# Cross-attention of a streaming encoder layer: queries projected features-first, and a fixed order for the passage to the products with wo

## The chip, the cores and the metric

The kernel runs on one core of a Trainium2 chip. The metric is the device time of one execution in microseconds (us); lower is better. Differences of less than 0.2% are taken as no change.

## The reference

One layer on 1024 tokens of width 1024, all in float32: a mixer (forgetting attention and gated linear attention side by side) with its output product w_out, a cross-attention to 256 memory tokens with 4 heads of 256, and an MLP with squared ReLU.

```python
h = h + parallel_mixer(rms_norm(h, norm_mix_g), w_in, ..., w_out)
h = h + memory_cross_attention(rms_norm(h, norm_xattn_g), rms_norm(mem, norm_mem_g),
                               xattn_wq, xattn_wkv, xattn_q_norm_g, xattn_k_norm_g, xattn_wo)
u = jax.nn.relu(rms_norm(h, norm_mlp_g) @ mlp_w1)
h = h + (u * u) @ mlp_w2

def memory_cross_attention(hn, memn, wq, wkv, q_norm_g, k_norm_g, wo):
    q = rms_norm((hn @ wq).reshape(B, S, XATTN_HEADS, XATTN_HEAD_DIM), q_norm_g)
    k, v = jnp.split(memn @ wkv, 2, axis=-1)
    k = rms_norm(k.reshape(B, M, XATTN_HEADS, XATTN_HEAD_DIM), k_norm_g)
    v = v.reshape(B, M, XATTN_HEADS, XATTN_HEAD_DIM)
    s = jnp.einsum('bshd,bmhd->bhsm', q, k) / math.sqrt(XATTN_HEAD_DIM)
    p = jax.nn.softmax(s, axis=-1)
    o = jnp.einsum('bhsm,bmhd->bshd', p, v).reshape(B, S, D_MODEL)
    return o @ wo
```

## The kernel before

Five engines work beside each other, each on its own list of instructions: TensorE (PE in the profile), VectorE (DVE), ScalarE (ACT), GpSimd (POOL), and SyncE (SP), which issues most transfers. The program is written in Python with pools of buffers; a scheduler that simulates the engines while the program is built sets the order of the instructions on each engine. An instruction waits on its engine until its operands are there and its output's buffer is free, and everything behind it on that engine waits with it.

Every float32 product is made of three products of halves. An operand is split into a high part (one copy on ACT) and a low part (operand minus high part, on DVE): `wh`, `wl` for weights, `sh`, `sl` for h, `th`, `tl` for the attention weights, `oh`, `ol` for the cross-attention's output. `gemm` (L105) then issues, for each block k of 128 summed features, high times high (L110), high times low (L111 or L112) and low times high. Where the text says "a product" of 128x512, one such PE instruction is meant.

The residual stream `h` lies in SBUF with features on the partitions: 8 blocks of 128 features, 1024 tokens each. `project_out` (L842) makes the last products with w_out, first for tokens 0 to 511 (half 0), then for half 1. For each of 8 feature blocks it loads `hr`, the part computed earlier, adds it on DVE (L860), squares the result on ACT (L169) and accumulates the squares on POOL (L170); `token_squares` (L172) sums the squares over features by four transposes on PE, and the token factors (among them `hev`) follow on POOL. After that comes `xattn` (L963), then `project_o_rest` (L891) with the rest of the products with wo, and `mlp`.

`xattn` works on half n of wq's columns (two heads) and a pair u of token tiles of 128:
- `weights(n)` loads half of wq in four transfers of 512 KB into two raw buffers and splits it (L99, L100), and loads the keys kT and values vm.
- `queries(n, u)` splits h of a token tile (`split_tile`, L823 and L824, one instruction each for 128x1024), and multiplies with the tokens as the stationary operand: 24 products 128x512. The result has tokens on the partitions, so `head_rstd` squares it on ACT, sums on DVE and takes the factor on POOL; DVE scales q, four transposes (L1003) turn it, and it is split into qh and ql.
- `attend(n, u)` makes for each token tile 12 score products 128x256, the maximum (DVE), the exponentials (ACT), the normalisation (POOL) and four transposes, and then for both tiles together 24 value products `pv` 128x256. The result `o` is split and stored to memory in four transfers of 256 KB (L1043).

The units run as (0,0) to (0,3), (1,2), (1,3), (1,0), (1,1); `attend` of a unit is written behind `queries` of the next. `project_o_first` (L883) loads o of half 1 in eight transfers of 512 KB (L872, L873), splits half of wo and makes four output blocks of 24 products.

Of the kernel before, what the change touches and what calls it, by code (L numbers as in the profile page):

```python
# [51 lines left out]
class Layer:  # L52
# [52 lines left out]
    def gemm(self, ps, lh, ll, rh, rl, start=True, stop=True, **kw):  # L105

        mm = self.nc.tensor.matmul
        n = len(lh)
        for k in range(n):
            mm(ps, lh[k], rh[k], start=start and k == 0, stop=False, **kw)  # L110
            mm(ps, lh[k], rl[k], start=False, stop=False, **kw)  # L111
            mm(ps, ll[k], rh[k], start=False, stop=stop and k == n - 1, **kw)  # L112
# [86 lines left out]
    def build(self):  # L199
        with ExitStack() as st:  # L200
# [19 lines left out]
            with ExitStack() as mx:  # L220
# [11 lines left out]
                self.h = self.T(self.open(st, "h", side="right"), [P, KT, S], F32, "h")  # L232
                self.project_out()
# [14 lines left out]
    def consts(self, cp):  # L248
# [9 lines left out]
        self.mhalf = self.T(cp, [P, 8], F32, "mhalf")  # L258
        nc.vector.memset(self.mhalf, -0.5)
# [554 lines left out]

    def split_tile(self, sp, srcs, kt=KT):

        nc = self.nc
        sh = self.T(sp, [P, kt, P], F32R, "sh")
        sl = self.T(sp, [P, kt, P], F32R, "sl")
        k = 0  # L820
        for src in srcs:
            w = src.shape[1]
            nc.scalar.activation(sh[:, k:k + w, :], src, AF.Copy)  # L823
            nc.vector.tensor_tensor(sl[:, k:k + w, :], src, f(sh[:, k:k + w, :]), ALU.subtract)  # L824
            k += w
        return [sh[:, k, :] for k in range(kt)], [sl[:, k, :] for k in range(kt)]

# [14 lines left out]
    def project_out(self):  # L842

        nc = self.nc
        with ExitStack() as st:
            banks = self.two(self.mmp, 2, self.open(st, "mm3b", 4, space=PSUM), 4)
            xp = self.open(st, "xp3", 3)
            self.acc = [self.T(xp, [P, 512], F32, f"acc{i}", bufs=1) for i in range(2)]
            ks = range(4), range(2, 4)
            Ws = [self.wsplit(self.w_out[ks[n][0] * P:512, n * 512:(n + 1) * 512], None, lo_pool=0) for n in range(2)]  # L850
            for half in range(2):
# [10 lines left out]
                c = slice(4 * half, 4 * half + 4)  # L862
                self.token_squares(half, self.hv[:, c])
                nc.gpsimd.tensor_scalar(self.hev[:, c], self.hv[:, c], EPS, None, ALU.mult)
                nc.gpsimd.tensor_tensor(self.hr[:, c], self.hv[:, c], self.mhalf[:, 0:4], ALU.pow)

    def load_o(self, op, half):

        oh = self.T(op, [P, KT, 512], F32R, "oh")
        ol = self.T(op, [P, KT, 512], F32R, "ol")  # L870
        for k in (slice(k, k + 2) for k in range(0, KT, 2)):
            self.nc.sync.dma_start(f(oh[:, k, :]), self.od[:, 0, half, k, :])  # L872
            self.nc.sync.dma_start(f(ol[:, k, :]), self.od[:, 1, half, k, :])  # L873
        self.O[half] = [oh[:, k, :] for k in range(KT)], [ol[:, k, :] for k in range(KT)]

    def o_block(self, W, n, half, i, ps, out=None):

        c = slice(i * P, (i + 1) * P)
        self.gemm(ps, *([w[:, c] for w in w_] for w_ in W), *self.O[half])
# [3 lines left out]
    def project_o_first(self):  # L883

        self.ost, self.O = ExitStack(), {}
        self.load_o(self.open(self.ost, "op0", side="right"), 1)
        self.Wo = self.wsplit(self.wo[:, 0:512], None)
        for i in range(4):
            self.o_block(self.Wo, 0, 1, i, self.T(self.mmp, [P, 512], F32, "mm"))

    def project_o_rest(self, mx):  # L891
# [5 lines left out]
        with ExitStack() as st:  # L897
            xp = self.open(st, "xp")
# [5 lines left out]
            op1 = self.open(st, "op1")  # L904
            wst = st.enter_context(ExitStack())
            wx = self.open(wst, "wx", 7)
            banks = self.two(self.mmp, 2, self.open(st, "mm5", 4, space=PSUM), 4)
# [3 lines left out]
            self.load_o(op1, 0)  # L911
# [3 lines left out]
            self.acc = [self.T(p, [P, 512], F32, "acc") for p in (self.open(mx, "acc", side="right"), xp)]  # L915
# [34 lines left out]
            self.A = next(self.W1)  # L950
# [12 lines left out]
    def xattn(self):  # L963
        nc = self.nc
        with ExitStack() as st:
            kvp = [None, self.open(st, "kv41")]
            qp = self.open(st, "q4", 3)
            qnp = self.open(st, "qn4", 2)
            pp = self.open(st, "p4", 3)
            ptp = self.open(st, "pt4", 2)  # L970
            mmp, trp = self.mmp, self.trp
            kst = ExitStack()
            kvp[0] = self.open(kst, "kv40")
            sst = ExitStack()
            sp = self.open(sst, "sp", 2, side="right")
            sps = self.open(st, "s4", 2, space=PSUM)
            pvp = self.open(st, "pv4", 2, space=PSUM)
            v2 = lambda ap: ap.rearrange("p (h d) -> p h d", h=2)
            v4 = lambda ap: ap.rearrange("p (h d) -> p h d", h=4)
            Ws, KV = {}, {}  # L980

            def weights(n):
                Ws[n] = self.wsplit(self.wq[:, n * 512:(n + 1) * 512], C_XAT)
                kT = self.T(kvp[n], [P, 2, 4, M], F32R, "kT")
                nc.sync.dma_start(f(kT), self.kTd[:, :, 4 * n:4 * n + 4, :])
                vm = self.T(kvp[n], [P, 2, 2, 512], F32R, "vm")
# [3 lines left out]
            def queries(n, u):  # L990
                qh = self.T(qp, [P, 2, 4, P], F32R, "qh")
                ql = self.T(qp, [P, 2, 4, P], F32R, "ql")
                for i in range(2):
                    t = 2 * u + i
                    A = self.split_tile(sp, (self.h[:, :, t * P:(t + 1) * P],))
                    ps = self.T(mmp, [P, 512], F32, "mm")
                    self.gemm(ps, *A, *Ws[n])
                    qn = self.T(qnp, [P, 512], F32, "qn")
                    r = self.head_rstd(ps, qn, 2, self.hev[:, t:t + 1])
                    nc.vector.tensor_tensor(v2(qn), v2(ps), self.bcast(r, 256), ALU.mult)  # L1000
                    tp = self.T(trp, [P, 512], F32, "tr")
                    for j in range(4):
                        nc.tensor.transpose(tp[:, j * P:(j + 1) * P], qn[:, j * P:(j + 1) * P], self.ident)  # L1003
                    self.evac_split(qh[:, i], ql[:, i], v4(tp))
                return qh, ql

            def attend(n, u, q):
                qh, ql = q
                kT, vm = KV[n]
                th = self.T(ptp, [P, 2, 4, P], F32R, "th")  # L1010
                tl = self.T(ptp, [P, 2, 4, P], F32R, "tl")
                for i in range(2):
                    ps = self.T(sps, [P, 512], F32, "s")
                    for h in range(2):
                        ks = (2 * h, 2 * h + 1)
                        self.gemm(ps[:, h * M:(h + 1) * M], [qh[:, i, k, :] for k in ks], [ql[:, i, k, :] for k in ks],
                                  [kT[:, 0, k, :] for k in ks], [kT[:, 1, k, :] for k in ks])
                    nm = self.T(self.smallp, [P, 2], F32, "nm2")
                    nc.vector.tensor_reduce(nm, v2(ps), AX.X, ALU.max, negate=True)
                    p = self.T(pp, [P, 512], F32, "p")  # L1020
                    rs = self.T(self.smallp, [P, 2], F32, "rs2")
# [26 lines left out]
            for i, (n, u) in enumerate(units):  # L1048
                if i % 4 == 0:
                    weights(n)  # L1050
# [301 lines left out]
```

## Time and profile before

| | |
|---|---|
| runs | 1447.37, 1449.64, 1446.28 us; median 1447.37 |
| profiled execution | 1445.83 us, of which the span (first to last instruction) 1444.0 us |
| granted TensorE clock, mean | 0.999 |
| busy: PE | 1423.1 us, 99% of the span |
| busy: PE weight loads (PEld) | 1186.4 us, 82% |
| busy: DVE, ACT, POOL | 946.0 us (66%), 680.1 us (47%), 395.3 us (27%) |
| DMA | 223.93 MB, mean 155 GB/s |

The cross-attention runs from about 587 to 750 us of the span. Busy shares are averages over the whole program; the weight loads run beside the products, so their share is not added to PE's. Rows of the profile name an instruction by its line, engine and operation, then output <- inputs with the program's names, the shape (partitions x elements), and a count; a bracket at the end of a timeline row gives the idle time ahead of the instruction and what ended it.

### The profile page before, as it was taken

What the parts mean: (1) busy time and instruction counts of PE and PEld (TensorE: products, weight loads), DVE (VectorE), ACT (ScalarE), POOL (GpSimd) and SP (SyncE); (2) the same over time, 40 slices, a digit from 0 to 9 for tenths busy, and PEclk for the clock granted to TensorE, in tenths of its full rate; (3) what the DMA queues carried; (4) which work ended last, traced back from release to release, by engine and by line L of the source; (5) the groups of instructions that cost most, each with busy time, mean ns of one, the idle gap of its engine ahead of it and who ended that gap; (6) DMA issues with size and microseconds to landing.
All of it is one profiled execution on the core that took longest, in us unless ns stands there. A gap on an engine that the chain in (4) does not pass through costs nothing.

```text
span 1444.0 us, 19212 instructions
## 1 busy us (share of the span) xinstructions
PE 1423.1 (99%) x7068; PEld 1186.4 (82%) x7068; DVE 946.0 (66%) x1342; ACT 680.1 (47%) x1095; POOL 395.3 (27%) x404
## 2 busy tenths in 40 slices
PE   9999999998999999999999999999999999999998
PEld 7788788886888887888888888888888888888887
DVE  5366732428788776666644896655556968788697
ACT  4444341327778565454542364445446645335230
POOL 4135513312242223422211300000000552233454
PEclk9999999999999999999999999999999999999999
DMA  8435620268677643412474114444446835336353
GB/s 279 126 78 127 140 68 1 74 177 259 199 222 233 192 132 88 131 59 89 160 275 156 51 71 181 157 175 189 175 175 223 325 108 190 131 128 222 119 199 120
DMA packets 121165, 223.93 MB, mean 155 GB/s; under 512 B 8912, under 2 KB 54512, under 8 KB 118512
## 3 DMA queue, kind: packets, MB, share of 16 engines
q1 hardware_dynamic: 119776, 218.25, 46.8%
q10 hardware_dynamic: 1296, 4.46, 1.0%
q8 instruction: 56, 0.92, 0.3%
q14 instruction: 37, 0.30, 0.1%
HBM read 150.59 MB, written 72.09 MB: 154 GB/s over the span
## 4 chain that ended last, share of the span: by engine, by line
PE 86%; DMA 6%; ACT 3%; DVE 3%; issue 1%; POOL 1%; ACTq 0%; SPq 0%; DVEq 0%
PE mm L110 14%; PE mm L112 14%; PE mm L111 14%; PE my L110 7%; PE my L112 7%; PE my L111 7%; PE tr L110 3%; PE tr L111 3%; PE tr L112 3%; PE tr L700 2%; DMA raw<-in_w_in_dram 1%; PE pv L708 1%; PE pv L707 1%; DMA xt<-in_x_dram 1%; PE s L660 1%
## 5 line engine op out<-in xcount | busy, mean ns | idle before, releaser
L110 PE MATMUL my<-x,g 128*128 128x512 f32 x464 | 180.7, 390 | 0.5 <-ACT h L1288 0.3
L111 PE MATMUL my<-x,g 128*128 128x512 f32 x464 | 180.6, 389 | 0.0
L112 PE MATMUL my<-x,g 128*128 128x512 f32 x464 | 180.5, 389 | 0.0
L111 PE MATMUL mm<-wl,xh 128*128 128x512 f32 x320 | 126.5, 396 | 0.9 <-DVE wl L100 0.8
L110 PE MATMUL mm<-wh,xh 128*128 128x512 f32 x320 | 126.0, 397 | 1.0 <-DVE sq L308 1.0
L112 PE MATMUL mm<-wh,xl 128*128 128x512 f32 x320 | 126.0, 394 | 0.0
L1080 ACT ACTIVATE g<-s 128x1024 fp32r<-128x1024 f32 (+1 forms) x72 | 69.1, 964 | 101.9 <-PE my L112 40.4
L1081 DVE TENSOR_TENSOR g<-raw,g 128x512 fp32r<-128x512 f32 (+3 forms) x72 | 68.9, 961 | 68.8 <-ACT g L1080 68.7
L1080 ACT ACTIVATE g<-raw 128x512 fp32r<-128x512 f32 (+3 forms) x72 | 55.5, 773 | 101.9 <-DMA raw<-in_mlp_w_dram 38.9
L1107 POOL TENSOR_TENSOR s<-raw 128x384 f32<-128x384 f32 (+1 forms) x20 | 26.3, 1315 | 280.4 <-DMA raw<-in_mlp_w_dram 244.5
L110 PEld LDWEIGHTS my<-x,g 128*128 128x128 f32 x464 | 87.1, 188 | 19.3 <-ACT h L1288 0.7
L111 PEld LDWEIGHTS my<-x,g 128*128 128x128 f32 x464 | 87.1, 188 | 18.2 <-DVE x L1081 0.2
L112 PEld LDWEIGHTS my<-x,g 128*128 128x128 f32 x464 | 87.1, 188 | 18.1
L671 POOL TENSOR_SCALAR p<-p,rrec 128x128 f32<-128x128 f32 (+3 forms) x64 | 57.4, 899 | 157.4 <-DVE rrec L670 153.2
L1081 DVE TENSOR_TENSOR g<-s,g 128x1024 fp32r<-128x1024 f32 (+1 forms) x72 | 87.5, 1218 | 8.8 <-ACT g L1080 8.8
L1250 DVE TENSOR_TENSOR x<-x 128x1024 fp32r<-128x1024 f32 (+1 forms) x64 | 75.7, 1203 | 16.4 <-ACT x L1249 16.2
L111 PE MATMUL mm<-x,g 128*128 128x512 f32 x220 | 85.7, 389 | 0.0
L110 PE MATMUL mm<-x,g 128*128 128x512 f32 x220 | 85.6, 389 | 0.0
L112 PE MATMUL mm<-x,g 128*128 128x512 f32 x220 | 85.6, 389 | 0.0
L110 PE MATMUL tr<-x,g 128*128 128x512 f32 x212 | 82.5, 389 | 0.0
L111 PE MATMUL tr<-x,g 128*128 128x512 f32 x212 | 82.5, 389 | 0.0
L112 PE MATMUL tr<-x,g 128*128 128x512 f32 x212 | 82.5, 389 | 0.0
(318 smaller groups left out, 3723.7 us busy)
## 6 DMA issues: line engine op xcount, KB each, us to landing
ud<-h SPq DMA_DIRECT2D x32, 768.0 KB, 3.8
x<-ud SPq DMA_DIRECT2D x48, 512.0 KB, 5.5
raw<-in_mlp_w_dram SPq DMA_DIRECT2D x20, 1024.0 KB, 7.3
raw<-in_mlp_w_dram SPq DMA_DIRECT2D x16, 768.0 KB, 5.9
raw<-in_w_in_dram SPq DMA_DIRECT2D x23, 512.0 KB, 4.6
raw<-in_xattn_wkv_dram SPq DMA_DIRECT2D x16, 512.0 KB, 8.0
od<-o SPq DMA_DIRECT2D x32, 256.0 KB, 4.1
ud<-h SPq DMA_DIRECT2D x32, 256.0 KB, 5.0
```

The lines of the kernel that those rows point to most:

```text
L110: mm(ps, lh[k], rh[k], start=start and k == 0, stop=False, **kw)
L111: mm(ps, lh[k], rl[k], start=False, stop=False, **kw)
L112: mm(ps, ll[k], rh[k], start=False, stop=stop and k == n - 1, **kw)
L660: nc.tensor.matmul(ps[:, c], qa[:, ts], ka[:, c], start=True, stop=False)
L671: nc.gpsimd.tensor_scalar(p[:, 0:n], p[:, 0:n], rr, 1.0, ALU.mult, ALU.mult)
L700: nc.tensor.transpose(o, pp[i][:, kb * P:(kb + 1) * P], self.ident)
L707: nc.tensor.matmul(pv, va[:, kb, :], th[:, js], start=kb == 0, stop=False)
L708: nc.tensor.matmul(pv, va[:, kb, :], tl[:, js], start=False, stop=kb == nb - 1)
L1080: a = self.nc.scalar.activation(hi, src, AF.Copy)
L1081: d = self.nc.vector.tensor_tensor(lo, src, f(hi), ALU.subtract)
L1107: eng.tensor_tensor(s[:, 0], raw[:, 3], raw[:, 2], ALU.add)
L1250: nc.vector.tensor_tensor(lo, f(lo), f(hi), ALU.subtract)
```

## The change

- Queries: a block of 128 columns of wq becomes the stationary operand and 512 tokens of h move, so q comes out with features on the partitions and isn't transposed. h is split in 128x512 pieces (`split`). Each pair of column blocks (one head) is squared on ACT and added on POOL; four transposes of the sum (L1010 in the new kernel) and a sum on DVE give the token sums, POOL the factor `rq`. q itself is not scaled: the factor enters the exponential as its scale.
- Units are half n of the columns and half of the tokens: (0,0), (0,1), (1,1), (1,0). `scores` and `transposed` work on a token tile as before; `values` makes for 512 tokens four groups `pv` of six 128x512 products each, in two PSUM banks, and stores each in one transfer of 512 KB. kT and vm have one buffer each, and the second half's load is called in the third unit.
- The first four feature blocks of o (half 1) are loaded while the last queries run; the other four follow as before.
- `h1_factors` of half 1 is called behind the second query block of the first unit.
- The passage: `issue_after(x)` makes the scheduler place the enclosed instructions behind x. Query (3,3), the last, stands behind values(2); then come scores, o_block 0, scores, transposes, o_blocks 1 and 2, values(3), o_block 3. The later load of W1 is placed behind the loads of o of half 0.

```diff
     def gemm(...)
-            mm(ps, ll[k], rh[k], start=False, stop=stop and k == n - 1, **kw)
+            end = mm(ps, ll[k], rh[k], start=False, stop=stop and k == n - 1, **kw)
+        return end.ins
...
+                self.acc1 = self.T(self.open(st, "acc", side="right"), [P, 512], F32, "acc")
                 self.project_out()
...
-                c = slice(4 * half, 4 * half + 4)
-                self.token_squares(half, self.hv[:, c])
...
+                if half == 0:
+                    self.h1_factors(half)
...
-    def load_o(self, op, half):
+    def load_o(self, op, half, ks):
...
     def xattn(self):
+            kvp = self.open(st, "kv4", **kw)
+            qp = self.open(st, "q4", 6, **kw)
...
+            def split(half, ks):
+                for k in ks:
+                    sh = self.T(sp, [P, 512], F32R, "sh")
+                    sl = self.T(sp, [P, 512], F32R, "sl")
+                    self.evac_split(sh, sl, self.h[:, k, half * 512:(half + 1) * 512])
...
+            def query(u, W, A, j):
+                ps = self.T(mmp, [P, 512], F32, "mm")
+                c = slice(j * P, (j + 1) * P)
+                end = self.gemm(ps, *([w[:, c] for w in w_] for w_ in W), *zip(*A))
+                q = self.T(qp, [P, 2, 512], F32R, "q")
+                self.evac_split(q[:, 0], q[:, 1], ps)
+                sq = self.T(sqp, [P, 512], F32, "sq")
+                nc.scalar.activation(sq, ps, AF.Square)
...
+                nc.gpsimd.tensor_tensor(sq, sq, self.sq0, ALU.add)
+                tp = self.T(trp, [P, 512], F32, "tr")
+                for t in range(4):
+                    self.sq_end = nc.tensor.transpose(tp[:, t * P:(t + 1) * P], sq[:, t * P:(t + 1) * P], self.ident).ins
...
+            def values(u):
+                for j in range(4):
+                    pv = self.T(pvp, [P, 512], F32, "pv")
+                    end = self.gemm(pv, *([vm[:, i, m, c] for m in range(2)] for i in range(2)),
+                              [th[:, m] for m in ms], [tl[:, m] for m in ms])
+                    o = self.T(pp, [P, 2, 512], F32R, "o")
+                    self.evac_split(o[:, 0], o[:, 1], pv)
+                    nc.sync.dma_start(self.od[:, :, half, 4 * n + j, :], f(o))
...
+            units = [(0, 0), (0, 1), (1, 1), (1, 0)]
+                for j in range(4):
+                    if j == 3 and u in (0, 2):
+                        A = split(units[u + 1][1], range(1))
+                    if u == j == 3:
+                        with self.tc.issue_after(values(u - 1)):
+                            end = query(u, W, keep, j)
+                        continue
+                    end = query(u, W, keep, j)
+                    if u == 0 and j == 1:
+                        self.h1_factors(1)
+                    if u and j == 0:
+                        if u == 3:
+                            self.load_o(op, 1, range(4))
+                        for t in range(4):
+                            transposed(u - 1, t, scores(u - 1, t)[0])
+                    elif 0 < u < 3 and j == 1:
+                        values(u - 1)
+                        if u == 2:
+                            memory(1)
...
+            self.load_o(self.open(self.ost, "op0b", side="right", **kw), 1, range(4, KT))
+            self.Wo = self.wsplit(self.wo[:, 0:512], None)
+            with self.tc.issue_after(end):
+                ps = [scores(3, t) for t in range(2)]
+            end = ps[-1][1]
+            for i in range(4):
+                with self.tc.issue_after(end), self.tc.issue_after(self.sq_end):
+                    end = self.o_block(self.Wo, 0, 1, i, self.T(self.mmp, [P, 512], F32, "mm"))
+                with self.tc.issue_after(end):
+                    if i == 0:
+                        ps += [scores(3, t) for t in range(2, 4)]
+                        end = ps[-1][1]
+                    if i < 2:
+                        for t in (2 * i, 2 * i + 1):
+                            transposed(3, t, ps[t][0])
+                    elif i == 2:
+                        end = values(3)
```

How the instructions stand at three places follows; the number behind a name tells one buffer from another. First ACT at the start of the queries, before: sqT are the squares of half 1, sh the first two split token tiles, wh the splits of wq.

```order
L169 ACTIVATE sqT_5983<-h_5805 128x512
L823 ACTIVATE sh_6226<-h_5805 128x1024
L823 ACTIVATE sh_6271<-h_5805 128x1024
L166 ACTIVATE acc_1376_5813<-h_5805 128x512
L169 ACTIVATE sqT_6045<-h_5805 128x512
L99 ACTIVATE wh_6196<-raw_6190,cols_74 128x512
```

The first two tiles stand ahead of all squares of half 1 (acc is the first of them, and the last comes further down). The same engine and place in the changed kernel:

```order
L99 ACTIVATE wh_6749<-raw_6747,cols_74 128x512
L170 ACTIVATE sqT_6125<-h_5805 128x512
L170 ACTIVATE sqT_6138<-h_5805 128x512
L118 ACTIVATE sh_6217<-h_5805 128x512
L118 ACTIVATE sh_6221<-h_5805 128x512
```

Now sqT_6138, the last square of half 1, stands ahead of sh_6217, the first split of the queries.

Second, PE where value products begin, before (a middle unit; tr of L1003 are transposes of a query, s scores):

```order
L112 MATMUL s_7435<-kT_6926,ql_7122 128x256
L1003 MATMUL tr_7351<-ident_75,qn_7342 128x128 x3
L110 MATMUL pv_7275<-th_7213,vm_6928 128x256
L110 MATMUL pv_7293<-th_7213,vm_6928 128x256
L1003 MATMUL tr_7351<-ident_75,qn_7342 128x128
L110 MATMUL s_7435<-kT_6926,qh_7121 128x256
```

And values(2), of the third unit, in the changed kernel (tr of L1052 are transposes of attention weights, which ACT and DVE split into th_7196 and tl_7197; the rows ahead are the products mm_7340 of the last query block but one):

```order
L1052 MATMUL tr_7260<-ident_75,p_7252 128x128 x4
L1052 MATMUL tr_7291<-ident_75,p_7283 128x128 x4
L110 MATMUL pv_7370<-th_7196,vm_7031 128x512
L110 MATMUL pv_7381<-th_7196,vm_7031 128x512
L1010 MATMUL tr_7329<-ident_75,sq_7326 128x128 x4
L111 MATMUL pv_7370<-tl_7197,vm_7031 128x512
```

Between the last transposes and the first value product stands nothing now; the next two groups are pv_7392 and pv_7403, then the last query block mm_7414.

Third, ACT in the passage of the changed kernel (o_7410 is the last of values(2), raw and wh are of wo, q_7439 and sq_7442 are the last query block and its squares):

```order
L118 ACTIVATE o_7410<-pv_7403 128x512
L88 ACTIVATE wh_7471<-raw_7465 128x512
L88 ACTIVATE wh_7477<-raw_7475 128x512
L88 ACTIVATE wh_7481<-raw_7475 128x512
L118 ACTIVATE q_7439<-mm_7414 128x512
L88 ACTIVATE wh_7487<-raw_7485 128x512
L88 ACTIVATE wh_7491<-raw_7485 128x512
L1003 ACTIVATE sq_7442<-mm_7414 128x512
```

The square stands behind two splits of raw_7485, whose load goes into the buffer that the splits of raw_7465 (wh_7471 on ACT, wl_7472 on DVE) leave free. PE at the same place:

```order
L112 MATMUL s_7505<-kT_7029,q_7439 128x256
L112 MATMUL s_7529<-kT_7029,q_7439 128x256
L1010 MATMUL tr_7445<-ident_75,sq_7442 128x128 x4
L110 MATMUL mm_7553<-oh_7166,wh_7467 128x512
L111 MATMUL mm_7553<-ol_7167,wh_7467 128x512
```

tr_7445 are the transposes of those squares, and o_block 0 (mm_7553) stands directly behind them. Before, output products and scores were mixed in this place:

```order
L112 MATMUL s_7625<-kT_6926,ql_7312 128x256
L110 MATMUL mm_7843<-oh_7793,wh_7805 128x512
L110 MATMUL s_7694<-kT_6926,qh_7501 128x256
L111 MATMUL s_7694<-kT_6926,qh_7501 128x256
L111 MATMUL mm_7843<-ol_7794,wh_7805 128x512
```

So where scores of one tile were made between output products before, all of the last query's factors now come ahead of the first output product.

More of the change, by code (lines that the diff above doesn't have):

```diff
@@ L847, in project_out @@
             xp = self.open(st, "xp3", 3)
-            self.acc = [self.T(xp, [P, 512], F32, f"acc{i}", bufs=1) for i in range(2)]
+            self.acc = [self.T(xp, [P, 512], F32, "acc", bufs=1), self.acc1]
             ks = range(4), range(2, 4)
@@ L876, in o_block @@
     def o_block(self, W, n, half, i, ps, out=None):
         c = slice(i * P, (i + 1) * P)
-        self.gemm(ps, *([w[:, c] for w in w_] for w_ in W), *self.O[half])
+        end = self.gemm(ps, *([w[:, c] for w in w_] for w_ in W), *self.O[half])
         h = self.h[:, 4 * n + i, half * 512:(half + 1) * 512]
         self.nc.vector.tensor_tensor(h if out is None else out, ps, h, ALU.add)
[L883 to L889, printed above, removed]
+        return end
@@ L910, in project_o_rest @@
             self.wps = wps
-            self.load_o(op1, 0)
+            loaded = self.load_o(op1, 0, range(KT))
             for i in range(4):
@@ L914, in project_o_rest @@
             self.ost.close()
[L915 removed]
+            self.acc = [self.acc1, self.T(xp, [P, 512], F32, "acc")]
             x0 = self.open(mx, "x0", 2, side="right", **kw)
@@ L949, in project_o_rest @@
             self.W1 = self.weights7([self.w1[q] for q in range(2)], 512, nc.vector, True)
-            self.A = next(self.W1)
+            with self.tc.issue_after(loaded):
+                self.A = next(self.W1)
             for i in range(4):
@@ L985, in weights @@
                 nc.sync.dma_start(f(kT), self.kTd[:, :, 4 * n:4 * n + 4, :])
-                vm = self.T(kvp[n], [P, 2, 2, 512], F32R, "vm")
+                vm = self.T(kvp, [P, 2, 2, 512], F32R, "vm")
                 nc.sync.dma_start(f(vm), self.vmd[:, :, :, n * 512:(n + 1) * 512])
                 KV[n] = kT, vm
[L990 to L1005, printed above, removed]
@@ new lines, in xattn @@
+            units = [(0, 0), (0, 1), (1, 1), (1, 0)]
+            A = []
+            for u, (n, half) in enumerate(units):
+                if u % 2 == 0:
+                    W = self.wsplit(self.wq[:, n * 512:(n + 1) * 512], C_XAT)
+                if u == 0:
+                    memory(0)
+                    A = split(half, range(KT))
+                keep = A
+                for j in range(4):
+                    if j == 3 and u in (0, 2):
[16 more added lines that the diff above has]
+                            memory(1)
+                if u in (0, 2):
+                    A = A + split(units[u + 1][1], range(1, KT))
```

171 lines of the change are left out of this document (83 added, 88 removed).

## The prediction

> **What bounds the kernel now.** I read the page's chain of waits first, then the windows of the stage that is rewritten, then the waits of TensorE (PE), then single rows of the timeline.
>
> ```profile
> PE 86%; DMA 6%; ACT 3%; DVE 3%; issue 1%; POOL 1%; ACTq 0%; SPq 0%; DVEq 0%
> 586.00:700.00 114.00, 114.00 (x654) 99.73 (x653) 70.53 (x106) 57.41 (x114) 30.63 (x54) 1.00 0.33 106
> 700.00:750.00 50.00, 48.70 (x310) 43.35 (x309) 28.81 (x50) 23.94 (x56) 9.23 (x18) 1.00 0.62 210
> 750.00:800.00 50.00, 50.00 (x232) 41.68 (x231) 25.23 (x37) 12.54 (x21) 11.17 (x9) 1.00 0.44 159
> PE mm L110 <- DMA oh<-od: 0.8, 1, 0.8
> PE mm L111 <- DMA ol<-od: 0.5, 2, 0.3
> ```
>
> The chain is 86% PE. In the windows (PE, PEld, DVE, ACT, POOL busy us, then granted clock, DMA share, GB/s), PE is busy all 114 us of the cross-attention up to 700 and all 50 us after 750; between them it misses 1.30 us. The two rows of PE's waits name those 1.3 us: three waits for the loads of the cross-attention's output o. So only two things can move the time here: how many PE cycles the stage needs, and how long PE stands. DVE (62%), ACT (50%) and POOL (27%) have room; they matter where PE waits for one of their results.
>
> The price of PE's work is the distance between starts, since the rows' own durations overlap:
>
> ```profile
> 586.57 0.39 PE L112 MATMUL mm<-sh,wl 128*128 128x512 f32 x1
> 586.80 0.39 PE L110 MATMUL mm<-wh,sh 128*128 128x512 f32 x1
> 587.02 0.39 PE L111 MATMUL mm<-wl,sh 128*128 128x512 f32 x1
> 587.25 0.39 PE L112 MATMUL mm<-wh,sl 128*128 128x512 f32 x1
> 664.87 0.28 PE L110 MATMUL pv<-th,vm 128*128 128x256 f32 x1
> 664.99 0.28 PE L111 MATMUL pv<-tl,vm 128*128 128x256 f32 x1
> 598.15 0.60 PE L1003 MATMUL tr<-ident,qn 128*128 128x128 f32 x4
> 598.51 0.48 PE L110 MATMUL mm<-wh,sh 128*128 128x512 f32 x1
> 598.83 0.39 PE L111 MATMUL mm<-wl,sh 128*128 128x512 f32 x1
> L1003 PE MATMUL tr<-ident,qn x64: 270/272/276, 598.2 to 726.8; 128*128 128x128 f32 x64
> ```
>
> A 128x512 product takes 0.227 us (586.80 to 587.25 is two), a 128x256 one 0.12, four transposes 0.36 (598.15 to 598.51), and the product after them another 0.09 (0.32 to the next instead of 0.23).
>
> **The sum, what is removed.** Query, score and output products keep their number and shape (618 of 128x512 and 192 of 128x256 between the last product with w_out and the MLP): the operands of the queries only change places. The 192 value products 128x256 (23.04 us) become 96 of 128x512 (21.76): -1.3. The 64 query transposes (row above) become 32 of the summed squares: eight groups of four fewer at 0.36 + 0.09, less one: -3.5. The waits for o: half of it is loaded during the queries, so -1.3 (between 0 and -1.3: the other half still comes late in the passage).
>
> **The start of the queries, +6.0.** At 586.57 PE made the last product with w_out, at 586.80 the first query product, with no gap, though the last additions and squares came later:
>
> ```profile
> 573.10 1.99 ACT L823 ACTIVATE sh<-h 128x1024 fp32r<-128x1024 f32 x2
> 590.48 0.63 ACT L169 ACTIVATE sqT<-h 128x512 f32<-128x512 f32 x1 [0.70 <-POOL acc L170]
> 591.74 0.63 ACT L169 ACTIVATE sqT<-h 128x512 f32<-128x512 f32 x1 [0.63 <-DVE h L860]
> 574.23 3.81 DVE L824 TENSOR_TENSOR sl<-h,sh 128x1024 fp32r<-128x1024 f32 x2 [0.63 <-ACT sh L823]
> 589.69 0.69 DVE L860 TENSOR_TENSOR h<-mm,hr 128x512 f32<-128x512 f32 x1 [2.53 <-DMA hr<-hpd]
> 590.30 0.74 DVE L100 SCALAR_TENSOR_TENSOR wl<-raw,cols,wh 128x512 fp32r<-128x512 f32 x1
> 590.96 0.68 DVE L860 TENSOR_TENSOR h<-mm,hr 128x512 f32<-128x512 f32 x1
> 591.56 1.55 DVE L100 SCALAR_TENSOR_TENSOR wl<-raw,cols,wh 128x512 fp32r<-128x512 f32 x1
> 591.25 3.01 POOL L170 TENSOR_TENSOR acc<-acc,sqT 128x512 f32<-128x512 f32 x2 [0.80 <-ACT sqT L169]
> 581.32 3.34 SPq L80 DMA_DIRECT2D raw<-in_xattn_wq_dram  x2
> 584.88 0.94 SPq L855 DMA_DIRECT2D hr<-hpd  x2
> ```
>
> Two token tiles stood split since 573 to 578, so PE had 48 products (10.9 us) in hand. In the new order the first split, sh_6217, stands on ACT behind both last squares (the fence in the section on the change), and nothing of the queries was split before. The last square waits for the last addition at 590.96, and that for hr, whose load stands on SP behind two raw loads of wq (issued 584.88, landed 589.69, 4.8 us). DVE loses the 3.81 us of sl ahead of these, but the splits of wq that free raw also wait for PE, so I take the addition 1.0 us earlier (estimate, 0.3 to 1.6): 590.0, its square 590.75, sh 591.4, PE 592.0. That is 5.2 after 586.80. The third product needs sl of the same tile, behind a wl of 0.74 alone or 1.55 beside POOL's accumulation (both rows above): about 593.2 against 587.25, so +6.0. From there the order lets PE make the products of two column blocks for each k (six, 1.36 us), and one split per k costs ACT 0.63 and DVE 0.69: no further wait. Lower end 2.5: hr lands before it is needed, and add 0.69, square 0.63, sh 0.63, sl 0.69 follow the last product directly (586.96 + 2.64 = 589.6 against 587.25). Upper end 7.5: 1.5 more for splits that queue behind POOL's two additions. I take 6.0, since the late hr stands in the row.
>
> The Trainium skill, "SBUF — State Buffer", section "Who interferes with whom", says that a DVE instruction with two SBUF inputs and a GpSimd instruction that reads SBUF exclude each other. The 1.55 us of wl agrees; sl has two SBUF inputs as well, so by the rule it would wait for the running addition and the term would be some 6.5.
>
> **The start of values(2), +1.35.** The order puts both groups of transposes directly ahead of pv_7370, and query (3,3) behind values(2). PE's first value product needs both th, which stand on ACT behind the evacuation of q_7365:
>
> ```profile
> L117 ACT ACTIVATE o<-pv x16: 592/597/607, 636.1 to 748.3; 128x512 fp32r<-128x512 f32 x16
> L118 DVE TENSOR_TENSOR o<-pv,o x16: 670/688/693, 637.4 to 749.5; 128x512 fp32r<-128x512 f32 x16
> od<-o SPq DMA_DIRECT2D x16, 256.0 KB, 2.4
> raw<-in_xattn_wo_dram SPq DMA_DIRECT2D x6, 512.0 KB, 3.7
> DMA to landing us min/median/max: 2.4/4.1/7.9
> ```
>
> From the start of the last query product: its end 0.39, then three evacuations of 0.60 with some 0.03 between, 2.3; PE could start at 0.227 + 0.72 = 0.95. Ends: 0 (ACT done in time) and 2.
>
> **Two banks for four value products, +1.2.** pv_7392 needs the bank of pv_7370: its end is 0.16 after the next start, then ACT 0.60, DVE 0.69 and two hand-overs of about 0.13 make 1.7, against five products (1.13): 0.6. The same in values(3): 1.2. Ends 0 and 2.4 (each of the four).
>
> **The wo load in the passage, +1.2.** Let 0 be the end of pv_7370's turn. PE comes to tr_7445 (squares of the last query) after 1.7 + 12 products (2.7) + 24 (5.4) + 24 of 0.12 (2.9): 12.75. ACT's square for it stands behind wh_7487 and wh_7491, which wait for raw_7485; that load's issue waits for wl_7472, whose wh stands behind the evacuation of o_7410 (done at 5.2). So wl at 6.7, load 3.7: 10.5, three of 0.63 on ACT: 12.4, POOL's addition 1.5 (3.01 for two): 13.9, which is 1.15 late. o_7410 also waits for the store of o_7377, which with 2.4 lands at 4.1, in time, with the median 4.1 over all loads 1.2 late. Ends 0.1 (no load in the way) and 5 (load of 7.9). I take 1.2, by the rows of these two transfers themselves.
>
> Costed at nothing: the rewritten chain of query factors (24 or more products lie between it and its exponentials), kT and vm of the second half (loaded some 20 us ahead), the later W1 load (DVE and ACT have room after 750, rows above), the squares on ACT (as many as before).
>
> Sum: -1.3 - 3.5 - 1.3 + 6.0 + 1.35 + 1.2 + 1.2 = +3.65. On the profiled execution's 1445.83 that is 1449.5; the median of the runs, 1447.37, stands 1.54 above it, so 1451.0.
>
> **Rivals.** (1) hr lands in time and the gap is 2.5: +0.15, 1447.5. For it: the load is only late because raw loads stand ahead, and DVE is freed ahead of them; against: the issue also waits for PE's use of the old weights. It decides when hr lands before 588. (2) The clock falls during the gap:
>
> ```profile
> 1.04 4.45 PE L292 MATMUL mm<-zerob 128*128 128x512 bf16 x10 [1.04 <-DVE mhalf L259]
> PE mm L393 <- ACT mixg L368: 1.9, 1, 1.9
> ```
>
> Ten products after PE's idle start took 4.45 us against 2.27: +2.2, so 1453.2. Against: the granted clock is 1.00 in the windows, but no stand of PE in this trace is longer than 1.9. The Trainium skill, "TensorE: Matmul & The Clock Gate", "What's actually happening", has an idle window of about 3.4 us halve the clock; a gap of 5 us can then halve it, and no row here shows such a gap. (3) The wo load takes its long time: +3.8 more, 1454.8. (4) Faster: the gap is 2.5 and ACT is on time at values(2) and in the passage (0, 0.1, and 0.6 for the banks): -6.1 + 2.5 + 0.7 = -2.9, and with the gap hidden altogether -5.4: 1444.5 to 1442.0, in the middle 1443.2. It ends on the other side when the first split is ready by 588. (5) Part of the change does nothing: the later four o loads are late as before (+1.3, 1452.3); it stays within the forecast.
>
> **How the numbers follow.** Forecast 0.45 (its own range 1449 to 1453; 0.35 of it above 1450.3); gap 2.5: 0.19; clock: 0.14; long load: 0.08; faster: 0.14. Less than 0.2% (2.9 us) can't be told from no change here. Slower by that: 0.35 + 0.14 + 0.08 = 0.57; same: 0.10 + 0.19 and a small part of the faster case, 0.30; faster 0.13. The range leaves out the faster case's greater part and the end of the long load: 1445.0 to 1455.0.
>
> **What would show it.** In the new trace PE should stand about 5 us before the first query product, released by ACT's sh and behind it DVE's addition with hr; about 1.3 before the first value product of the third unit, released by ACT's th; 0.6 before the third value product there, released by DVE's o; about 1 before the last transposes of squares, released by POOL; the granted clock stays 1.00. A first query product less than 1 us after the last one with w_out would make the forecast wrong.

## The result: 0.5% slower, twice what was forecast

| kernel | runs | median us | lowest to highest |
|---|---|---|---|
| before | 6 | 1448.51 | 1446.28 to 1451.27 |
| changed | 6 | 1457.23 | 1454.36 to 1459.47 |

The ratio is 1.0053, 95% interval 1.0038 to 1.0068. The three runs of the kernel before that the prediction started from (median 1447.37) were on the low side: over 67 executions in the later comparisons its median is 1450.17 (1444.57 to 1454.44). The changed kernel, run again six times, had 1457.70.

The waits of PE in the changed kernel between 580 and 800 us (waited for, total us, times, longest):

```profile
PE mm L110 <- ACT sh L118: 5.1, 1, 5.1
PE tr L1010 <- POOL sq L1007: 2.4, 1, 2.4
PE pv L110 <- ACT th L118: 0.8, 1, 0.8
PE pv L110 <- DVE o L119: 0.6, 2, 0.3
PE mm L111 <- DVE sl L119: 0.3, 1, 0.3
```

The waits for loads of o are gone; in their place are the five waits that the prediction placed. The windows of the same stretch, and a finer one behind the start of the queries (PE, PEld, DVE, ACT, POOL, granted clock, DMA share, GB/s):

```profile
586.00:700.00 114.00, 108.54 (x550) 91.58 (x549) 58.45 (x101) 56.88 (x114) 34.02 (x49) 0.97 0.27 86
700.00:750.00 50.00, 46.50 (x254) 39.60 (x253) 22.43 (x47) 22.59 (x56) 13.42 (x24) 1.00 0.50 179
594.00:602.00 8.00, 7.65 (x21) 5.54 (x21) 5.97 (x9) 3.77 (x8) 0.61 (x1) 0.59 0.09 35
```

From 594 to 602 PE is busy nearly throughout and yet makes 21 products where 35 fit: the granted clock is 0.59. PE's timeline of the changed kernel shows where that begins and ends:

```profile
588.16 0.39 PE L112 MATMUL mm<-sh,wl 128*128 128x512 f32 x1
593.66 1.21 PE L110 MATMUL mm<-sh,wh 128*128 128x512 f32 x2 [5.11 <-ACT sh L118]
595.21 0.79 PE L111 MATMUL mm<-sl,wh 128*128 128x512 f32 x1 [0.35 <-DVE sl L119]
595.80 0.63 PE L112 MATMUL mm<-sh,wl 128*128 128x512 f32 x1
596.23 0.63 PE L110 MATMUL mm<-sh,wh 128*128 128x512 f32 x1
600.07 0.61 PE L110 MATMUL mm<-sh,wh 128*128 128x512 f32 x1
600.50 0.42 PE L111 MATMUL mm<-sl,wh 128*128 128x512 f32 x1
600.75 0.39 PE L112 MATMUL mm<-sh,wl 128*128 128x512 f32 x1
```

After the last product with w_out (588.16) PE stands for 5.1 us. Then products come at 0.43 us instead of 0.227 until about 600.5, apart from a wait for sl ahead of the third. The sixteenth product starts at 600.75, 7.09 after the first; at full pace and without a wait it would be 3.40.

Executions also differ ahead of the change, so a difference of whole executions mixes two things. A stretch with the same landmarks in both kernels holds the change alone: from the transposes of the squares of half 0 (5.93 us before the start of the last product with w_out in both) to those of the token factors ahead of the last output blocks. First the kernel before, then the changed one:

```profile
580.64 0.60 PE L177 MATMUL tr<-ident,acc 128*128 128x128 f32 x4
759.03 1.95 PE L189 MATMUL tr<-sB,onesq 128*128 128x128 f32 x16
```

```profile
582.23 0.60 PE L178 MATMUL tr<-ident,acc 128*128 128x128 f32 x4
767.47 1.95 PE L190 MATMUL tr<-sB,onesq 128*128 128x128 f32 x16
```

The stretch takes 178.39 us before and 185.24 changed: +6.85, where the sum said +3.65. From 759.03 and 767.47 to the ends of the spans it is 685.0 and 685.1: nothing is gained or lost behind it. The 1.6 us by which the changed kernel is late at the first landmark arise between 330 and 384 us, where both kernels still run the same instructions in the same order (see the last section).

The split of the 6.85: the first query product comes 5.27 us later than right behind the last w_out product (593.66 - 588.16 - 0.23). The third, the first that needs sl, starts at 595.21 instead of 588.84 and is 6.37 late, so sl adds 1.10. The sixteenth is 8.96 late (600.75 - 588.16 - 16 times 0.227): from the third to the sixteenth the low clock adds 2.59. Everything after that gives back 2.11.

### The profile page after: what moved, and what is told of

Its sections match the earlier page's. It is cut to its first block, busy times and chain, and to the rows that moved or that the text cites. A ratio compares the mean times of both kernels' runs of the same rounds, so it can differ in the third digit from the quotient of the medians.

```text
span 1452.6 us, 18893 instructions
## 1 busy us (share of the span) xinstructions
PE 1424.4 (98%) x6940; PEld 1181.6 (81%) x6940; DVE 932.5 (64%) x1342; ACT 681.3 (47%) x1103; POOL 399.0 (27%) x404
## 4 chain that ended last, share of the span: by engine, by line
PE 84%; DMA 7%; ACT 3%; DVE 3%; issue 2%; POOL 1%; SPq 0%; ACTq 0%; DVEq 0%
PE mm L110 14%; PE mm L111 14%; PE mm L112 14%; PE my L110 7%; PE my L112 7%; PE my L111 7%; PE tr L112 3%; PE tr L111 3%; PE tr L110 3%; PE tr L703 2%; PE pv L711 1%; PE pv L710 1%; DMA raw<-in_w_in_dram 1%; DMA xt<-in_x_dram 1%; PE s L663 1%
## 5 line engine op out<-in xcount | busy, mean ns | idle before, releaser
L110 PE MATMUL mm<-sh,wh 128*128 128x512 f32 x256 | 103.3, 406 | 5.6 <-ACT sh L118 5.1
L112 PE MATMUL mm<-sh,wl 128*128 128x512 f32 x256 | 102.5, 401 | 1.9 <-DVE wl L93 1.9
L111 PE MATMUL mm<-sl,wh 128*128 128x512 f32 x256 | 102.1, 400 | 0.3 <-DVE sl L119 0.3
```

The lines of the kernel that those rows point to most:

```text
L112: end = mm(ps, ll[k], rh[k], start=False, stop=stop and k == n - 1, **kw)
```

## The experiments

In what follows "the stretch" is the one between those two landmarks, 178.39 before and 185.24 changed, and "the start" is the lateness of the sixteenth query product, 0 before and 8.96 changed. Each is read from one profiled execution. Each kernel is an edit of the changed one unless it says otherwise.

**The first splits early.** Why does the first split stand so late? The new pools `op0a` and `sp` lie on the right side of SBUF one below the other, and `sp` so reaches onto the memory in which project_out keeps its `hr` loads. The profile shows no addresses, but it does show what the instructions wait for: the first split, whose operand h comes from DVE, waits for the signals that five transfers have landed, each a signal that a load of hr was the last to use (the latest issued at 585.50), and the scheduler puts it behind the squares. With sp opened first the first split waits for no transfer, and ACT gets all eight splits of the first half ahead of the last squares. The last four blocks of o now go into sp's buffers, in eight smaller transfers.

```diff
-            op = self.open(self.ost, "op0a", side="right", **kw)
-            sst = ExitStack()
-            sp = self.open(sst, "sp", 9, side="right", **kw)
+            sp = self.open(self.ost, "sp", 9, side="right", **kw)
+            op = self.open(self.ost, "op0a", side="right", **kw)
...
-            self.load_o(self.open(self.ost, "op0b", side="right", **kw), 1, range(4, KT))
+            for k in range(4, KT):
+                for i, n in enumerate(("sh", "sl")):
+                    t = self.T(sp, [P, 512], F32R, n)
+                    nc.sync.dma_start(f(t), self.od[:, i, 1, k, :])
+                    self.O[1][i].append(t)
```

> The changed kernel with the split pool sp opened ahead of op0a, so that the first splits of the queries no longer lie on the memory of the late hr loads; the scheduler then puts the eight splits of the first half ahead of the last squares on ACT, as before the change. The last four feature blocks of o are loaded into sp's buffers by eight transfers of 256 KB instead of four of 512 KB. Theory (the late first split makes the 5.1 us wait of PE, and that wait makes the low clock behind it): the first query product starts within 0.5 us of the last product with w_out, the granted clock stays 1.00 from 586 to 610, and 8.5 us go (about 5.3 for the wait, 0.4 for sl, 3 for the clock): some 1446 where the changed kernel has 1454.4 and 1450 where it has 1459, 1.5 to 2.5 us below the kernel before. Rival (the clock falls for another reason than the wait, such as the new operand order): the wait goes, the clock is still 0.5 for some 7 us, and only 5.5 go. Rival (the weights of wq are late too and were hidden by the wait): PE waits for wh or wl instead, 2 to 4 us remain.

Measured: 1450.03 us against 1450.48 before, ratio 0.9998 (0.9983 to 1.0012). PE at the same place, then the window behind it:

```profile
588.97 0.39 PE L112 MATMUL mm<-sh,wl 128*128 128x512 f32 x1
590.45 0.50 PE L110 MATMUL mm<-sh,wh 128*128 128x512 f32 x1 [1.09 <-DVE h L849]
594.00:602.00 8.00, 8.00 (x37) 6.35 (x36) 4.13 (x5) 2.94 (x6) 4.17 (x4) 1.00 0.21 72
```

The wait for sh is gone and the clock stays 1.00. The stretch takes 178.58 (583.04 to 761.62), 6.66 less than in the changed kernel: practically the whole loss lay here. The start is 1.39 instead of 8.96. Not the full 8.5 came back: 1.25 us are left ahead of the first query product, which waits for a PSUM bank that DVE's addition of a late hr frees (the nine low parts now stand ahead of these additions on DVE), and a new wait of 1.4 us for exp appeared in the passage.

**PE kept busy in the wait.** The same kernel as the changed one, with products of zeros in the gap.

```diff
+            warm = self.T(self.mmp, [P, 512], F32, "mm")
+            with self.tc.issue_after(end):
+                for _ in range(22):
+                    self.filled = self.nc.tensor.matmul(
+                        warm, self.zerob, self.zerob.unsqueeze(1).to_broadcast([P, 4, P]), start=True, stop=True).ins
```

> The changed kernel with 22 products 128x512 of zeros (bf16, into a bank that nobody reads) behind the last product with w_out, about 5 us of PE work that is of no use. Theory (an idle PE makes the clock fall): the first query product starts at the same distance of 5.3 to 5.6 us, but the granted clock stays 1.00, and 3 us go: some 1451.4 where the changed kernel has 1454.4. Rival (the clock falls for another reason): the clock is 0.5 from about 594 to 601 all the same and the time stays. Rival (the fill itself delays the queries): the first query product comes later than 5.6 us after the last one with w_out, and less than 2 us go.

Measured: 1454.34 us against 1450.48, ratio 1.0032 (1.0013 to 1.0051). PE and the windows at that place:

```profile
594.38 4.92 PE L856 MATMUL mm<-zerob 128*128 128x512 bf16 x22
600.26 0.73 PE L110 MATMUL mm<-sh,wh 128*128 128x512 f32 x2 [0.96 <-ACT sh L118]
601.88 0.50 PE L111 MATMUL mm<-sl,wh 128*128 128x512 f32 x1 [0.88 <-DVE sl L119]
594.00:602.00 8.00, 6.16 (x28) 2.60 (x27) 5.72 (x7) 5.78 (x11) 6.38 (x5) 1.00 0.41 139
```

The first query product still comes 6.1 us after the last w_out product (594.15), 0.6 more than in the changed kernel, but the clock is 1.00. The stretch takes 183.49, 1.75 less. That is under 2 us behind a distance over 5.6, as the last alternative had it; but the unaltered kernel run once more (below) has the same distance, so the fill need not be what made it longer. The operands came later: the third product is 7.04 late instead of 6.37. From the third product to the sixteenth only 0.13 are added instead of 2.59, so the clock is worth 2.5 here, somewhat less than the 3 expected. The low clock comes from PE's standing still, not from the new order of operands.

**The same loss put into the kernel before.** One edge in the kernel before, nothing of the change.

```diff
+                    if n == 0 and u == 0:
+                        with self.tc.issue_after(self.last_sq):
+                            A = self.split_tile(sp, (self.h[:, :, t * P:(t + 1) * P],))
```

> The kernel before with one edge: the splits of the first two token tiles stand on ACT behind the last square of half 1, as the first split does in the changed kernel. Nothing else of the change is in it. Theory (a split behind the late hr load makes PE wait, and that wait the low clock): PE waits some 6 us ahead of its first query product (the split is one instruction of 128x1024 here, so ACT takes 1.0 and DVE 1.9), the granted clock falls to 0.5 for about 7 us behind it, and the kernel is 9 to 11 us slower than before. Rival (the clock falls only with queries computed features-first): the wait comes, the clock stays 1.00, 6 to 7 us slower.

Measured: 1458.30 us against 1450.10, ratio 1.0058 (1.0041 to 1.0076).

```profile
585.67 0.39 PE L112 MATMUL mm<-sh,wl 128*128 128x512 f32 x1
591.69 0.79 PE L110 MATMUL mm<-wh,sh 128*128 128x512 f32 x1 [5.63 <-ACT sh L823]
588.00:589.00 1.00, 0.00 (x0) 0.00 (x0) 1.00 (x2) 0.38 (x1) 0.82 (x1) 0.73 0.00 0
595.00:596.00 1.00, 1.00 (x5) 0.83 (x4) 0.44 (x1) 0.00 (x0) 0.39 (x2) 0.86 0.00 0
```

The wait and the low clock appear with tokens stationary too, and by the medians the whole is as much slower as the change (+8.2, under the 9 to 11 expected). The profiled execution was the fastest of the nine, 1451.37. Its stretch is 184.80 (+6.41): here the clock fell earlier, at 588.5 (0.73 over the window of 588 to 589), while PE still waited, and was back at 595.3. Of 6.8 us of half clock PE had 3.6 to work in, so 1.8 were lost. With the 5.79 by which the first product is late that makes 7.6. Part of the difference to 6.41 is seen: the 1.3 of waits for o are gone from this profile, and a wait of 0.7 for exp is new.

**The changed kernel once more.**

> The changed kernel unaltered, to see how much its executions differ. Theory (the low clock behind the wait at the start of the queries comes every time, its cost hangs on where the wait ends): the wait is again 5.0 to 5.6 us, the granted clock is 0.5 for 5 to 7 us behind it, and the part from the transposes of half 0's squares to those of the token factors ahead of the last output blocks takes 183.5 to 185.5 us against 178.4 before; what else differs between executions lies ahead of the queries. Rival (the wait itself differs by microseconds between executions): it leaves 4.5 to 6.

Measured: 1457.70 against 1450.08, ratio 1.0049 (1.0034 to 1.0064). PE waited 5.77 us for sh, the start is 9.43, the stretch took 185.90 (585.78 to 771.68). The wait was a little above the stated 5.6, the stretch 0.4 above its bound. The window of the low clock:

```profile
597.34:604.17 6.83, 5.91 (x13) 4.23 (x14) 6.74 (x10) 4.61 (x9) 1.46 (x1) 0.50 0.21 73
```

The wait and the low clock stand in both profiles of the changed kernel, and in the two of the kernels below that leave its start as it is. The stretch differs by 0.66 between two profiles of one kernel, so a difference of that size between kernels says little.

**wo's splits behind the squares.** One edge on ACT.

```diff
-            self.Wo = self.wsplit(self.wo[:, 0:512], None)
+            self.Wo = self.wsplit(self.wo[0:512, 0:512], None)
+            with self.tc.issue_after(self.sq_act):
+                self.Wo = [a + b for a, b in zip(self.Wo, self.wsplit(self.wo[512:1024, 0:512], None))]
```

> The changed kernel with the splits of the second half of wo's first columns put behind the squares of the last query on ACT (one edge in the order, nothing else). Theory (the square stood behind two splits that wait for a wo load): PE's wait of 2.4 us for POOL's sum of squares shrinks to under 0.6, and about 2 us go. Rival (the load is needed next anyway): o_block 0 waits at its ninth group for wh of the same load instead, and the time stays within 0.5 us.

First the chain in the changed kernel that this cuts (SP's issue of raw, ACT's splits and square, POOL's addition, PE):

```profile
725.69 1.74 SPq L80 DMA_DIRECT2D raw<-in_xattn_wo_dram  x2
731.19 1.15 ACT L88 ACTIVATE wh<-raw 128x512 fp32r<-128x512 f32 x2 [1.51 <-DMA raw<-in_xattn_wo_dram]
732.24 0.58 ACT L1003 ACTIVATE sq<-mm 128x512 f32<-128x512 f32 x1
732.90 1.37 POOL L1007 TENSOR_TENSOR sq<-sq,sq 128x512 f32<-128x512 f32 x1 [12.51 <-ACT sq L1003]
734.32 0.66 PE L1010 MATMUL tr<-ident,sq 128*128 128x128 f32 x4 [2.41 <-POOL sq L1007]
```

And PE with the edge:

```profile
731.58 0.66 PE L1010 MATMUL tr<-ident,sq 128*128 128x128 f32 x4 [0.59 <-POOL sq L1007]
737.12 0.50 PE L111 MATMUL mm<-ol,wh 128*128 128x512 f32 x1 [0.55 <-DMA ol<-od]
```

The wait shrank from 2.41 to 0.59; a load of o became late by 0.55 in its place. The stretch is 182.80, 2.44 less, but not all of that is the edge's. In this profile the clock fell earlier, while PE still waited for its first split:

```profile
591.13:594.12 2.99, 0.00 (x0) 0.00 (x1) 2.89 (x5) 1.83 (x4) 2.24 (x3) 0.50 0.20 49
```

So the start is 7.52 instead of 8.96, and 1.44 of the 2.44 lie there; 1.0 is left for the edge, half of the 2 expected. The median of the runs, 1456.34, can't tell that from the changed kernel's 1457.

**Without the edge at values(2).**

```diff
-                        with self.tc.issue_after(values(u - 1)):
-                            end = query(u, W, keep, j)
+                        values(u - 1)
+                        end = query(u, W, keep, j)
```

> The changed kernel without the edge that puts the last query block behind values(2). Theory (the edge leaves PE nothing between the last transposes and the first value product): PE's wait of 0.8 us for th goes, with the restart about 1.2 us, and the two waits of 0.3 for a bank of values(2) may stay. Rival (o of values(2) and with it the output blocks come later, since its products now stand among the scores): PE waits as long for oh or ol in o_block 0, 1 to 4 us, and the kernel is no faster or slower.

Measured: 1467.07 us, ratio 1.0116 (1.0088 to 1.0144); the rival held, and worse than stated. PE's waits from 700 to 760, and the window:

```profile
PE mm L110 <- DMA oh<-od: 7.9, 2, 5.1
PE mm L111 <- DMA ol<-od: 1.1, 2, 0.7
700.00:750.00 50.00, 40.95 (x207) 33.66 (x206) 18.55 (x39) 17.76 (x44) 11.59 (x20) 0.86 0.51 170
```

The wait for th is gone, but values(2) now ends among the scores, o is stored later, and o_block 0 waits 9 us for it; the clock falls there as well (0.86 over the window). The edge that I charged with 1.35 us saves far more than it costs.

**Two edits together, and then two more.** Early splits with wo's splits late:

> The splits of the first half early and the splits of wo behind the last squares, both edits in one kernel. Theory: the gains add, the wait for POOL's sum stays under 0.6 and the wait of 1.45 us of the third score group for exp goes, since exp no longer stands behind splits that wait for wo: 1.5 to 2.5 us less than with the early splits alone, some 1.5 us (0.1%) below the kernel before, within what can be told from no change. Rival (the output blocks wait for wo or o instead): no gain over the early splits.

Measured: 1448.92 us against 1450.10, ratio 0.9997 (0.9985 to 1.0010), the stretch 178.65. The gains did not add: PE's wait for POOL's sum is 0.6 with the early splits alone already, so the late splits of wo had nothing left to shorten there. The wait for exp did not go:

```profile
734.19 0.39 PE L110 MATMUL s<-kT,q 128*128 128x256 f32 x1 [1.45 <-ACT p L1038]
```

Then five buffers for hr, and the last query block cut in two with `held` its values(2):

```diff
-                    hr = self.T(xp, [P, 512], F32, "hr")
+                    hr = self.T(xp, [P, 512], F32, "hr", bufs=5)
...
+                    self.gemm(ps, *(v[:2] for v in ops), stop=False)
+                    with self.tc.issue_after(held()):
+                        end = self.gemm(ps, *(v[2:] for v in ops), start=False)
```

> As the one before, with five buffers for hr instead of three (its loads are issued earlier) and with only the last 18 of the 24 products of the last query block behind values(2), so that the first six can stand between the last transposes and the first value product. Theory: the wait of 1.1 us for the addition with hr ahead of the first query product goes, and the 0.8 us ahead of the first value product too, with the restarts about 2.3 us less: some 4 us (0.25%) below the kernel before. Rival (hr is late because DVE's additions stand behind splits of wq, not for want of a buffer): the 1.1 us stay, 1.2 us less.

Measured: 1450.35 us, ratio 1.0009 (0.9995 to 1.0023), the stretch 177.92. The 0.98 us ahead of the first query product stayed, as the rival said: the additions stand on DVE behind splits, and more buffers don't help. The value products still waited 0.46 for th and 0.70 for tl: six products are too little cover.

Last, with twelve products ahead of values(2), and the low parts of the first splits (from the third on) behind the sixth addition on DVE:

```diff
+                    add = nc.vector.tensor_tensor(h, ps, hr, ALU.add).ins
...
+                    A = split(half, range(2))
+                    with self.tc.issue_after(self.add_bank):
+                        A = A + split(half, range(2, KT))
```

> As the last but one of these kernels (early splits, wo's splits late, five hr buffers, part of the last query block ahead of values(2)), with 12 instead of 6 of its products ahead of values(2) and with the low parts of the first splits from the third on behind the addition of the sixth block on DVE, so that they don't hold up the additions that free the bank of the first query product. Theory: the 1.0 us ahead of the first query product goes, and the 0.5 and 0.7 at values(2): 2 to 2.5 us less than without, the part between the two transposes some 176 us, 2.5 us (0.17%) under before, which runs may not tell from no change. Rival (the low parts now come late for PE): PE waits for sl 1 to 3 us instead and nothing is gained.

Measured: 1445.53 us (12 runs) against 1450.08 (16 runs), ratio 0.9970 (0.9956 to 0.9983): 0.3% faster than before (by the interval 0.2 to 0.4), and faster than the changed kernel. PE's waits from 586 to 760:

```profile
PE mm L111 <- DMA sl<-od: 1.6, 1, 1.6
PE pv L110 <- DVE o L119: 0.7, 2, 0.3
PE tr L1016 <- POOL sq L1013: 0.6, 1, 0.6
```

The stretch takes 176.10 (584.61 to 760.71), 2.29 less than before, as expected. The start is 0. The medians differ by 4.5; the other 2 us do not show in the stretch of this one profile and are not explained. The last four blocks of o are still 1.6 late.

## Why the prediction was right and wrong

The direction and the places were right; the size was not: +3.65 forecast, +6.85 in the stretch. Nearly all of that lies at the start, 8.96 instead of 6.0; what follows was forecast at -2.35 in sum and came to -2.11.

- **The start of the queries, +6.0: the step that failed.** The wait came as worked out: the new last addition started at 591.69 and its square at 592.46, sh at 592.99, PE at 593.66, 5.27 late (5.2 stated); the third product, which needs sl, 6.37 late (6.0 stated). So the term was right for what it counted. What failed is that it ended there: it let the sixteen products behind the wait run at full pace and put the clock at nothing. The rows of DVE, ACT and POOL (the last one gives the shortest, median and longest ns of the nine sl):

```profile
590.11 0.69 DVE L849 TENSOR_TENSOR h<-mm,hr 128x512 f32<-128x512 f32 x1 [2.13 <-DMA hr<-hpd]
591.69 0.68 DVE L849 TENSOR_TENSOR h<-mm,hr 128x512 f32<-128x512 f32 x1
592.46 0.63 ACT L170 ACTIVATE sqT<-h 128x512 f32<-128x512 f32 x1 [0.94 <-DVE h L849]
592.99 4.77 ACT L118 ACTIVATE sh<-h 128x512 fp32r<-128x512 f32 x9
593.23 1.38 POOL L171 TENSOR_TENSOR acc<-acc,sqT 128x512 f32<-128x512 f32 x1 [0.31 <-ACT sqT L170]
593.64 1.52 DVE L119 TENSOR_TENSOR sl<-h,sh 128x512 fp32r<-128x512 f32 x1 [0.17 <-ACT sh L118]
L119 DVE TENSOR_TENSOR sl<-h,sh x9: 675/677/1518, 593.6 to 599.3; 128x512 fp32r<-128x512 f32 x9
```

What I left out of the sum and gave a chance of 0.14 as a rival, the fall of the clock, belongs to the same step: in each of the five profiles in which PE stood for 5.1 to 5.8 us and did nothing, 6.8 us of half clock followed, and the fill of zeros showed that it is the standing still. It cost 2.59 here, near the 2.2 of the rival. I weighed it low because no row showed such a gap; but a forecast that itself makes a gap longer than any in the trace can't take its clock from a trace without one. The Trainium skill, "TensorE: Matmul & The Clock Gate", section "What's actually happening", states an idle window of about 3.4 us, after which the clock is half, and a window that runs free of the kernel's start. The traces agree with the length and with the free window: each low clock lasted 6.8 us, twice 3.4 (593.7 to 600.5 and 588.5 to 595.3 in two of the profiles), and it began anywhere from 2.1 to 5.3 us after PE stopped. In the changed kernel's profile it fell at 334.30 and at 593.71, 76 times 3.413 apart. The traces don't agree with a window that is idle throughout: where the clock fell 2.1 to 2.7 us after PE stopped (three of the five profiles), the 3.4 us ahead of its fall held work as well.
- **The rule on shared reads.** The prediction also named a rule of the Trainium skill ("SBUF — State Buffer", section "Who interferes with whom"), by which the first sl would wait for POOL's running addition and the term would be some 6.5. The trace agrees with it. The first sl took 1.52 us, from 593.64, where the median of the nine is 0.68; POOL's addition ran from 593.23 to 594.61, and sl was done 0.55 behind it, at 595.16. With 6.37 measured, the 6.5 by the rule was nearer than the 6.0 taken.
- **Values(2), +1.35.** The wait for th is 0.79; from the end of the eight transposes (714.94 + 0.72) to the first value product it is 1.1. Right.

```profile
714.94 1.04 PE L1052 MATMUL tr<-ident,p 128*128 128x128 f32 x8
716.77 0.73 PE L110 MATMUL pv<-th,vm 128*128 128x512 f32 x2 [0.79 <-ACT th L118]
720.60 0.50 PE L110 MATMUL pv<-th,vm 128*128 128x512 f32 x1 [0.30 <-DVE o L119]
```

- **Two banks, +1.2.** Waits of 0.30 and 0.33; with the restart 0.47 in the row above (720.60 instead of 720.13), so some 0.9.
- **The wo load, +1.2: mis-sized.** 2.41. wl was done when I said; the load took 5.5 us from its issue at 725.69 to the split at 731.19, not 3.7. Two wo loads are issued together there, behind four stores of 512 KB; that this made it longer was not tested.
- **The waits for o, -1.3.** None is left in the changed kernel. Right, and the experiment without the edge shows how near it is.
- **The shorter work.** By difference: what follows the start gives back 2.11; with 1.1 + 0.9 + 2.5 of new waits and the 1.3 of o, 5.3 are left for value products and transposes, where 4.8 were counted. Not measured by itself. The prediction's count of 618 products of 128x512 should be 768 (384 of the queries and 384 with wo); no term of the sum uses it.
- **The base.** The runs shown had a median of 1447.37, some 2.8 below what the kernel before has over many runs; that is the rest of the way from 1451.0 to 1457.2. My range took no account of it. Either error alone, the clock's 2.6 or these 2.8, would have left the time below the upper end of 1455.0.

## What to carry to other kernels

Where a change opens a new gap on PE, price the gap and then the clock behind it: where PE stood for 5.1 to 5.8 us, the start came 7.5 to 9.4 us late here. Look at where new pools lie in memory and not only at what an instruction computes: a split that needed nothing late was made to wait for a load into old buffers, and swapping the order of two pools gave back 6.7 of 6.85 us. Before taking out an ordering edge that shows a small wait, ask what it holds early: here it kept a store ahead of nine microseconds of waiting.

## What the hardware showed that was not expected

- Behind the long wait the low clock lasted 6.8 us in all five profiles, but its beginning lay 2.1 to 5.3 us after PE stopped. So much the same wait cost PE between 1.1 us more (where the clock fell early in the wait, wo's splits behind the squares) and 2.6 (the changed kernel).
- A second place has a low clock by chance: between 330 and 345 us several PE waits of 0.2 to 1.9 us lie close together, each shorter than the 5 us above. The granted clock of that window was 1.00 in the profile before, 0.77 and 0.66 in the two profiles of the changed kernel, 0.89 with the fill. The kept profiles show shorter falls at other places too, near 60, 160 and 533 to 539 us, each in some of the kernels only. This can explain part of the spread of about 10 us between executions of the same kernel; how much was not measured. The profile that the prediction read happened to show none of it. In the changed kernel's profile PE is 0.14 us behind the kernel before at 330, 1.3 at 338 and 1.6 at 384; that is the 1.6 of the first landmark.

```profile
330.00:345.00 15.00, 11.85 (x48) 8.72 (x49) 14.37 (x28) 11.27 (x25) 5.57 (x4) 0.77 1.05 341
335.44 0.80 PE L112 MATMUL mm<-sh,wl 128*128 128x512 f32 x1 [1.92 <-DVE wl L93]
```

These two rows are of the changed kernel, window and PE, some 230 us ahead of the first instruction that the change moves.
